# Issue order of weight transfers in a decoder step: the next chunk's sum ahead of a further chunk's load

## The chip, the cores and the metric

The kernel runs on one core of a Trainium2 chip. The metric is the device time of one execution in microseconds (us). Several executions are timed, and the median counts. One more execution is recorded by the hardware profiler; all rows shown here are from such a recording.

The names are those of the profile: PE is the matrix engine, with PEld for its weight loads; DVE, ACT and POOL are the vector, scalar and GpSimd engines; SP is the engine that here only issues transfers. SPq and POOLq are transfers issued by SP and POOL. L191 is line 191 of the kernel before.

## The reference, cut to what matters

The reference is one inference step of a two-layer decoder for 512 prompt tokens and 8 sample tokens, all in fp32, with model width 1024. Each layer is

```
x = x + 0.5 * swiglu(rmsnorm(x), w_gate, w_up, w_down)
x = x + mixer(rmsnorm(x))        # layer 0: causal pooling, layer 1: window attention
x = x + 0.5 * swiglu(rmsnorm(x), w_gate, w_up, w_down)
swiglu(h) = (silu(h @ w_gate) * (h @ w_up)) @ w_down      # 1024 -> 2816 -> 1024
```

The keys and values of the attention are projected once from x after layer 0. The four feed-forward blocks (FFN 0 to 3) are nearly all of the work and hold nearly all of the weights.

## The kernel before, in words

All 520 tokens are kept on the chip as columns, in two halves of 260. The weights stream through once. For the precision of fp32, every weight block is split into a high and a low part: ACT writes the high part `wh` (L260), DVE writes the rest `wl` (L261), and a product is three matmuls, high times high, high times low and low times high, each of 128 x 128 by 260 columns. L533 is the matmul of plain tiles, L561 that of Strassen tiles.

An FFN has 22 tiles of 128 hidden columns, in parts of 8, 8 and 6. After each part its share of the down projection follows. The first tiles of every FFN (4, 3, 2 and 3) are plain. The other tiles take one step of Strassen's scheme (in Winograd's form): seven products instead of eight. The up and gate blocks of the tile are the two rows of a 2 x 2 matrix of weight blocks, and the seven products need four sums of such blocks: S1 = A21 + A22, S2 = S1 + A11, S4 = A12 + S2 in this kernel's signs, S3 = A11 + A21. The second parts of FFN 0 and FFN 1 also do their down projection so ("woven", because the pieces of neighbouring tiles alternate; 4 tiles of two column blocks each). All other down projections are plain, in 4 chunks.

The weights come through the class `Weights` in a plan written out ahead: a list of chunks (up to 1 MB each, one tile or one pair of column blocks) and a list of pieces in the order in which PE uses them. `_split` walks along the pieces, some five ahead of PE (`prefetch`):

- `load(c)` issues the transfers of chunk c from DRAM into one of 3 buffers `raw`, on SP. The buffer's previous user must be done.
- `add_up(c)` does the sums of a chunk which transfers can do (`loaded`, L187 to L192); for plain chunks it does nothing. On SP it loads one 256 KB block of the chunk a second time, into a tile S (4 rotating buffers, which some other tiles use too). On POOL it issues two accumulating transfers: L191 adds a block of `raw` to S, giving S1, and L192 adds A11 to A21 in place, giving S3. L191 must wait for the load of S and for that of the chunk, L192 for the chunk alone.
- DVE forms S2 (L197, which reads S) and S4 (L201) in place when their piece comes.
- Then ACT and DVE split the piece (L260, L261), and `_split` issues the load of a further chunk and the sum of the next one (L263 to L265).

`held` is true where one of the next two pieces still belongs to an earlier chunk; this is so at the Strassen tiles, whose last piece (A22) is used only after the next tile has begun. `slow` holds the second tile of a woven down projection.

The order of instructions on each engine isn't only that of the program: the framework schedules the instructions by a timeline of its own, within the limits of their dependences. The weight loads are pinned to the order of the program (`later`), as are some other instructions.

The lines to know beside these are: L317 and L318, the high and low part of activations; L332, the issue of every weight transfer on SP; L694 to L706, ACT's and DVE's copies and sums `sa` and `sb` in a Strassen tile; L725 to L752, the same in a woven down projection; L1220 to L1235, the copies of the new keys and values (`vtok` among them) at the start of FFN 2; L1355 to L1500, the attention, of which L1412 transposes the softmax.

Of the kernel before, what the change touches and what calls it, by code (L numbers as in the profile page):

```python
# [126 lines left out]
class Weights:  # L127
# [113 lines left out]
    def _split(self, i):  # L241
        nc = self.nc
        while self.ns <= min(i, len(self.items) - 1):
            it = self.items[self.ns]
            self.load(it[0])
            self.add_up(it[0])
            src = it[1](self.chunks[it[0]][1])
            n = src.shape[1]
            if it[2] is not None:
                dh, dl = it[2]()  # L250
                wh = wl = None
            else:
                wh = self.splp.tile([P, 4, P], F32R, tag="wh", name="wh")
                wl = self.splp.tile([P, 4, P], F32R, tag="wl", name="wl")
                dh, dl = wh[:, :n, :], wl[:, :n, :]
            if len(src.shape) == 4:
                dh = dh.rearrange("p k (e d) -> p k e d", e=2)
                dl = dl.rearrange("p k (e d) -> p k e d", e=2)
            pin = self.pin if wh is not None else self.pin_home
            pin(nc.scalar.activation(dh, src, AF.Copy))  # L260
            pin(nc.vector.tensor_tensor(dl, src, dh.bitcast(F32), op=ALU.subtract))  # L261
            it[2] = (wh, wl)
            held = any(c < it[0] for c, _, _ in self.items[self.ns + 1 : self.ns + 3])  # L263
            self.load(it[0] + self.ca - held)
            self.add_up(it[0] + 1 - (held and it[0] in self.slow))  # L265
            self.ns += 1

    def get(self):
# [1591 lines left out]
```

## Time and profile before

| | before |
|---|---|
| median of 3 runs | 1685.05 us (1684.97 to 1687.89) |
| profiled execution | 1681.19 us |
| its span, first to last instruction | 1679.4 us |
| granted PE clock, mean | 0.994 |
| HBM read | 182.40 MB, 112 GB/s over the span |
| SP's loads of raw, gate | x87, 512 KB, median 4.0 us from issue to landing |
| SP's loads of raw, up | x87, 512 KB, median 5.7 us |
| SP's loads of S | x76 of 256 KB from w_up, 5.6 us |
| POOL's accumulations L192 (raw) | x84, 256 KB, 3.4 us |

How to read the rows: in a timeline the columns are start (us from the first instruction), duration, engine, line, operation, tiles written and read, and in brackets the idle time of the engine just before, with what ended it. In the waits, a row names the waiting engine and line, then what it waited for, the total, the times and the longest. In a row by stretch (start:end) follow its length, then for PE, PEld, DVE, ACT and POOL the busy time and the number of instructions, the granted PE clock as a share of full speed, the share of the transfer engines and GB/s. A transfer that POOL or SP issues takes little of the issuing engine's time, unless the engine has to wait first.

### The profile page before, as it was taken

Reading aid. Unit: us, or ns where it says so; the run is one execution under the profiler, and the core shown is the slowest. Engines: PE = TensorE matmul, PEld = TensorE weight load, DVE = VectorE, ACT = ScalarE, POOL = GpSimd, SP = SyncE. Lnnn points to the kernel's source line nnn. Section 1 sums busy time; section 2 is a strip of 40 time slices with the busy share of each in tenths; the row PEclk is TensorE's granted clock in tenths of the full one; section 3 lists DMA queues with packets and bytes.
Section 4 is the critical chain, followed back from the end, with each engine's and each line's share of the span. In section 5 each row is a group of like instructions: output and inputs, shape, how many; then the busy total and the mean of one; then the engine's idle time right before and its main releaser. Section 6 shows DMA issues by size and latency. Waiting matters only on the chain.

```text
span 1679.4 us, 34587 instructions
## 1 busy us (share of the span) xinstructions
PE 1648.1 (98%) x13674; PEld 1634.9 (97%) x13674; DVE 1287.0 (77%) x2475; ACT 909.9 (54%) x1834; POOL 179.9 (11%) x240
## 2 busy tenths in 40 slices
PE   9999999999999999999999999999989999999997
PEld 9999999999999999999999999999989999999997
DVE  6866989887875998888775875886787785785776
ACT  5643655556652664655552552655785653463455
POOL 0101111000101111100201101101210100110100
PEclk9999999999999999999999999999999999999999
DMA  8646768752655777743755755653222554674641
GB/s 215 139 121 137 175 167 176 178 163 79 139 147 133 173 167 172 167 132 93 172 146 133 167 154 133 151 154 85 66 52 76 133 139 132 146 176 127 147 122 52
DMA packets 329646, 232.27 MB, mean 138 GB/s; under 512 B 10494, under 2 KB 303078, under 8 KB 329444
## 3 DMA queue, kind: packets, MB, share of 16 engines
q1 hardware_dynamic: 300414, 179.96, 38.1%
q0 software_dynamic: 25312, 45.02, 16.3%
q10 hardware_dynamic: 3758, 5.09, 1.0%
q8 instruction: 107, 1.75, 0.5%
q14 instruction: 55, 0.45, 0.1%
HBM read 182.40 MB, written 5.04 MB: 112 GB/s over the span
## 4 chain that ended last, share of the span: by engine, by line
PE 89%; DVE 3%; ACT 3%; DMA 2%; issue 2%; SPq 0%; POOL 0%; ACTq 0%; DVEq 0%; POOLq 0%
PE ps L561 47%; PE ps L533 36%; DMA S<-raw 1%; DVE wl L261 1%; DMA pr<-in_bands_dram 1%; PE ps L1075 1%; PE ps L1443 1%; DMA S<-in_ffn_w_down_dram 1%; ACT sm L1387 1%; ACT wh L260 1%; PE ps L1050 0%; PE ps L1412 0%; PE ps L1734 0%; ACT xh L317 0%; PE ps L1355 0%
## 5 line engine op out<-in xcount | busy, mean ns | idle before, releaser
L260 ACT ACTIVATE wh<-raw 128x512 fp32r<-128x512 f32 (+1 forms) x746 | 447.5, 621 | 455.6 <-PE ps L533 255.8
L261 DVE TENSOR_TENSOR wl<-raw,wh 128x512 fp32r<-128x512 f32 (+1 forms) x746 | 491.5, 677 | 164.5 <-ACT wh L260 161.4
L561 PE MATMUL ps<-th,wh 128*128 128x260 f32 x1216 | 344.4, 283 | 1.8 <-ACT sa L699 0.8
L561 PE MATMUL ps<-tl,wh 128*128 128x260 f32 x1216 | 342.7, 282 | 0.0
L561 PE MATMUL ps<-th,wl 128*128 128x260 f32 x1216 | 340.9, 282 | 0.2 <-DVE wl L261 0.2
L561 PEld LDWEIGHTS ps<-th,wh 128*128 128x128 f32 x1216 | 228.5, 188 | 3.5 <-DVE sb L706 1.4
L561 PEld LDWEIGHTS ps<-tl,wh 128*128 128x128 f32 x1216 | 229.0, 188 | 0.0
L561 PEld LDWEIGHTS ps<-th,wl 128*128 128x128 f32 x1216 | 227.9, 188 | 0.4 <-DVE wl L261 0.4
L533 PE MATMUL ps<-hh,wh 128*128 128x260 f32 x1084 | 219.2, 284 | 0.6 <-ACT vtok L1230 0.6
L533 PE MATMUL ps<-hl,wh 128*128 128x260 f32 x1084 | 219.1, 282 | 0.0
L533 PE MATMUL ps<-hh,wl 128*128 128x260 f32 x1084 | 217.7, 282 | 0.0
L192 POOL DMA_DIRECT2D raw<-raw x84 | 72.4, 862 | 1207.5 <-DVE wl L261 431.7
L561 PE MATMUL ps<-xh,wh 128*128 128x260 f32 x704 | 198.0, 283 | 0.5 <-ACT sb L696 0.5
L561 PE MATMUL ps<-xl,wh 128*128 128x260 f32 x704 | 197.5, 282 | 0.0
L561 PE MATMUL ps<-xh,wl 128*128 128x260 f32 x704 | 195.0, 282 | 0.0
L533 PEld LDWEIGHTS ps<-hh,wh 128*128 128x128 f32 x1084 | 166.5, 188 | 1.5 <-ACT vtok L1230 0.9
L533 PEld LDWEIGHTS ps<-hl,wh 128*128 128x128 f32 x1084 | 167.5, 188 | 0.0
L533 PEld LDWEIGHTS ps<-hh,wl 128*128 128x128 f32 x1084 | 167.0, 188 | 0.0
L533 PE MATMUL ps<-xl,wh 128*128 128x260 f32 x736 | 149.7, 284 | 0.3 <-DVE xl L949 0.3
L533 PE MATMUL ps<-xh,wh 128*128 128x260 f32 x736 | 149.1, 285 | 0.0
L533 PE MATMUL ps<-xh,wl 128*128 128x260 f32 x736 | 148.1, 283 | 0.0
L561 PEld LDWEIGHTS ps<-xh,wh 128*128 128x128 f32 x704 | 132.4, 188 | 0.9 <-ACT sb L696 0.9
(325 smaller groups left out, 3186.8 us busy)
## 6 DMA issues: line engine op xcount, KB each, us to landing
raw<-in_ffn_w_gate_dram SPq DMA_DIRECT2D x87, 512.0 KB, 4.0
raw<-in_ffn_w_up_dram SPq DMA_DIRECT2D x87, 512.0 KB, 5.7
raw<-in_ffn_w_down_dram SPq DMA_DIRECT2D x24, 1024.0 KB, 4.8
raw<-raw POOLq DMA_DIRECT2D x84, 256.0 KB, 3.4
S<-raw POOLq DMA_DIRECT2D x84, 256.0 KB, 4.4
S<-in_ffn_w_up_dram SPq DMA_DIRECT2D x76, 256.0 KB, 5.6
raw<-in_ffn_w_down_dram SPq DMA_DIRECT2D x16, 768.0 KB, 4.4
raw<-in_ffn_w_down_dram SPq DMA_DIRECT2D x32, 256.0 KB, 3.9
```

The lines of the kernel that those rows point to most:

```text
L192: G.dma_start(blk(raw, 2, 1), blk(raw, 1, 1), accum_op=ALU.add)
L260: pin(nc.scalar.activation(dh, src, AF.Copy))
L261: pin(nc.vector.tensor_tensor(dl, src, dh.bitcast(F32), op=ALU.subtract))
L533: ins = T.matmul(banks[:, hf, :H], a[:, kk, :], hcols(b, hf), start=(first and i == 0), stop=(last and i == 2),)
L561: T.matmul(bank[:, :H], a[:, kk, :], b, start=(not more and kk == 0 and i == 0), stop=(kk == 3 and i == 2), skip_group_check=more,)
L1075: T.matmul(po[:, half * 256 : half * 256 + 256], z[:, tau, c], b, start=(i == 0), stop=(i == len(lst) - 1),)
L1387: S.activation(z, z, AF.Exp, scale=-1.0, bias=nm[:, i : i + 1], accum_out=self.den[:, i : i + 1])
L1443: T.matmul(po[:, bi * 256 : (bi + 1) * 256], a, p_[:, kc_], start=(n == 0), stop=(n == 3 * len(kts) - 1),)
```

## The change

In `_split` the sum of the next chunk is asked for before the load of the further chunk, except that a sum is never asked for before its own chunk has been loaded (the `min`); what that leaves over is asked for behind the load, as before.

```diff
             held = any(c < it[0] for c, _, _ in self.items[self.ns + 1 : self.ns + 3])
+            sums = it[0] + 1 - (held and it[0] in self.slow)
+            self.add_up(min(sums, self.nl - 1))
             self.load(it[0] + self.ca - held)
-            self.add_up(it[0] + 1 - (held and it[0] in self.slow))
+            self.add_up(sums)
             self.ns += 1
```

The instructions are the same. Between Strassen tiles the sum stands ahead of the load already, since `held` puts the load off. What moves are 22 of the 84 sums: two at each of the ten places where plain chunks give way to Strassen chunks, and one, that of the third tile, in each of the two woven down projections. Around a change from plain to Strassen chunks, SP's order was load c+1, S of c, load c+2, S of c+1, S of c+2; it is S of c, load c+1, S of c+1, load c+2, S of c+2. On POOL, L191 of a moved sum goes ahead of L192 of the next chunk. In the woven projections the S of the third tile goes ahead of the four transfers that load the fourth. The framework's schedule also moves some instructions of ACT, DVE and PE: within and behind the woven projections, at the starts of FFN 1 and FFN 2, and in the attention.

## The prediction

> **What bounds the kernel now.** I read the page first, then PE's waits grouped by line, then all instructions on the tiles named S (the block of weight sums), then the timelines of the places where PE's waits lead.
>
> ```profile
> span 1679.4 us, 34587 instructions
> PE 1648.1 (98%) x13674; PEld 1634.9 (97%) x13674; DVE 1287.0 (77%) x2475; ACT 909.9 (54%) x1834; POOL 179.9 (11%) x240
> PE 89%; DVE 3%; ACT 3%; DMA 2%; issue 2%; SPq 0%; POOL 0%; ACTq 0%; DVEq 0%; POOLq 0%
> S<-raw POOLq DMA_DIRECT2D x84, 256.0 KB, 4.4
> ```
>
> PE's waits (us in total, times, longest), and from the view of S how long and how often an instruction on S sat idle for that transfer:
>
> ```profile
> PE ps L561 <- ACT wh L260: 2.4, 3, 1.9
> PE ps L561 <- DVE raw L197: 2.3, 1, 2.3
> PE ps L561 <- ACT sa L699: 0.8, 2, 0.6
> PE ps L561 <- DVE sb L706: 0.8, 2, 0.5
> DMA S<-raw: 44.7, 14
> ```
>
> PE is busy 1648.1 of 1679.4 us, and the change neither adds nor removes an instruction. The last row of the first fence gives 4.4 us from issue to landing for the accumulating transfer. So only PE's 31.3 idle us, and any time at a lower clock, can be won; everything else could only be lost. The two largest waits of the Strassen matmuls (L561) end with a split (L260) and with the sum S2 (L197), both readers of an S tile. The last row says that instructions on S tiles sat idle 14 times for S<-raw. There are 84 such transfers and the change moves 22 of their loads. Of these 22 the timelines of ACT and DVE show a split that starts when its S lands at three places only: 252.69, 643.75 and 808.14. The other moved sums lie 3 us or more in front of their splits, or PE does not wait.
>
> **The first place, FFN 0's woven down projection** (timelines of SP, POOL, ACT and PE; columns are start and duration, and the bracket is the idle time before it and its releaser):
>
> ```profile
> 230.21 13.39 SPq L332 DMA_DIRECT2D raw<-in_ffn_w_down_dram  x8
> 241.58 2.02 SPq L332 DMA_DIRECT2D raw<-in_ffn_w_down_dram  x4
> 243.64 1.58 SPq L332 DMA_DIRECT2D S<-in_ffn_w_down_dram  x2
> 249.13 0.86 POOL L191 DMA_DIRECT2D S<-raw  x1 [1.74 <-DMA S<-in_ffn_w_down_dram]
> 252.69 0.63 ACT L260 ACTIVATE wh<-S 128x512 fp32r<-128x512 f32 x1 [7.83 <-DMA S<-raw]
> 251.19 0.28 PE L561 MATMUL ps<-ph,wl 128*128 128x260 f32 x1
> 253.38 0.39 PE L561 MATMUL ps<-hh,wh 128*128 128x260 f32 x1 [1.91 <-ACT wh L260]
> 255.03 0.28 PE L561 MATMUL ps<-hh,wl 128*128 128x260 f32 x1
> 235.00:245.00 10.00, 10.00 (x86) 10.00 (x85) 9.74 (x19) 6.84 (x15) 0.86 (x1) 1.00 0.41 98
> ```
>
> The third tile's sum is queued on SP behind the fourth tile's load (four transfers, issued only at 241.58, when a raw buffer comes free). It therefore starts at 243.64; POOL can accumulate onto it at 249.13, ACT splits at 252.69, and PE stops. At full work PE does 86 matmuls in 10 us, 0.116 each. From 251.19 to 255.03 it makes 7 steps in 3.84 us: 7 x 0.116 = 0.8, so **3.0 us** are lost.
>
> The change puts this sum ahead of the fourth tile's load. It waits then for nothing that is late: it follows the first four transfers of the x8 row, about 230.2 + 2.0 = 232.2. With the same lags (243.64 to 249.13 is 5.5; L191 to landing 4.4 by the page) it has landed by about 242.5, nine us before PE needs it. The load behind it starts at 241.58 as before, since the buffer, not SP, holds it.
>
> **The second place, FFN 1's woven down projection:**
>
> ```profile
> 620.92 13.41 SPq L332 DMA_DIRECT2D raw<-in_ffn_w_down_dram  x8
> 634.38 1.23 SPq L332 DMA_DIRECT2D S<-in_ffn_w_down_dram  x2
> 640.38 1.75 POOL L191 DMA_DIRECT2D S<-raw  x2 [2.31 <-DMA S<-in_ffn_w_down_dram]
> 643.75 0.63 ACT L260 ACTIVATE wh<-S 128x512 fp32r<-128x512 f32 x1 [8.18 <-DMA S<-raw]
> 641.88 0.28 PE L561 MATMUL ps<-ph,wl 128*128 128x260 f32 x1
> 644.44 0.39 PE L561 MATMUL ps<-hh,wh 128*128 128x260 f32 x1 [2.28 <-DVE raw L197]
> 645.10:648.50 3.40, 3.32 (x14) 3.02 (x15) 3.40 (x7) 1.12 (x3) 0.00 (x0) 0.50 0.25 68
> 648.50:651.90 3.40, 3.40 (x31) 3.40 (x30) 2.80 (x6) 2.84 (x7) 0.00 (x0) 1.00 1.14 309
> ```
>
> It is the same pattern, and a second loss follows. From 641.88 to 645.10 PE starts 4 matmuls in 3.2 us: 3.2 - 4 x 0.116 = 2.75 lost. Then the granted clock is 0.50 for 3.4 us, with 14 matmuls against 31 in the next 3.4: 17 x 0.11 = 1.9 lost. Together **4.6 us**. Here an idle stretch of 2.28 us was followed by the half clock; at 253.38 one of 1.91 us was not.
>
> [...]
>
> **Knock-on.** Behind the woven stretch of FFN 0 the next tiles' sums stay late:
>
> ```profile
> 311.06 0.63 ACT L260 ACTIVATE wh<-S 128x512 fp32r<-128x512 f32 x1 [3.49 <-DMA S<-raw]
> 313.05 0.39 PE L561 MATMUL ps<-th,wh 128*128 128x260 f32 x1 [0.60 <-ACT sa L699]
> 317.73 0.39 PE L561 MATMUL ps<-th,wh 128*128 128x260 f32 x1 [0.55 <-DVE sb L706]
> ```
>
> The two L699/L706 waits (0.8 + 0.8 in PE's waits) and the pipeline refills behind them come to at most 2.7 us. These chunks' loads wait for the split of an A22 piece two chunks back, which comes earlier after the change. The transfers there are themselves slower than the 4.4 median, so lateness may build up again. Bounds 0 and 2.7; I take **1.0**, nearer to nothing because the cause, crowded transfers, isn't removed.
>
> **The 20 other sums (ten places where plain tiles give way to Strassen tiles).**
>
> ```profile
> L332 SPq DMA_DIRECT2D S<-in_ffn_w_up_dram x76: 557/1094/2763, 35.6 to 1594.8; - x76
> ```
>
> Each takes some 1.1 us of SP (the median of that row, of 0.56 to 2.76) ahead of a chunk's load, and its POOL accumulate goes ahead of the next chunk's L192. No row of PE's waits ends with a raw load; the loads have that much to spare, so I count nothing; (d) below is the price if they had not. But the scheduler orders ACT and DVE by its own estimate, and in two stages their order changes.
>
> *FFN 2's start.* The split of S goes ahead of the two copies L1230, for which PE waits:
>
> ```profile
> 782.12 0.37 SPq L332 DMA_DIRECT2D raw<-in_ffn_w_gate_dram  x1
> 794.29 1.51 SPq L332 DMA_DIRECT2D S<-in_ffn_w_up_dram  x1
> 800.96 1.21 POOL L191 DMA_DIRECT2D S<-raw  x1
> 799.32 0.58 ACT L1230 COPY vtok<-ps 128x512 f32<-128x512 f32 x1 [0.21 <-PE ps L1229]
> 801.48 0.51 PE L533 MATMUL ps<-hh,wh 128*128 128x260 f32 x2 [0.62 <-ACT vtok L1230]
> 808.14 0.63 ACT L260 ACTIVATE wh<-S 128x512 fp32r<-128x512 f32 x1 [4.51 <-DMA S<-raw]
> ```
>
> After the change this sum is issued behind the load at 782.12, near 783.2, not at 794.29: 11.1 us earlier, so the S that was ready at 808.14 should be ready at about 797, or earlier, before ACT reaches the split at 799. PE then waits some 0.63 (the split) longer, with its refill **+0.8** (bounds 0 and 9.4, the latter below).
>
> *Attention.* A split of the queries (L317/L318) moves behind other work where ACT and DVE are the limit:
>
> ```profile
> 1233.03 1.30 PE L1412 MATMUL ps<-ident,sm 128*128 128x128 f32 x5 [1.15 <-ACT oT L1462]
> 1232.20:1239.00 6.80, 5.97 (x32) 5.69 (x34) 6.49 (x22) 6.40 (x19) 1.61 (x2) 0.50 0.00 1
> ```
>
> I followed the new order by hand with the durations of the rows: about **+0.7** at the matmul of 1233.03. The stretch at half clock may move with it, so bounds are -1.5 and +2.5.
>
> **Sum**, against the profiled execution (1681.19 us, span 1679.4 and 1.8 around it): -3.0 - 4.6 - 1.0 + 0.8 + 0.7 = -7.1, 1674.1. That execution lies 3.86 below the median of the runs, 1685.05, so the forecast for the median is **1678.0** (-0.4%).
>
> **Rivals.**
>
> *(a) Half is given back to DVE.*
> ```profile
> 245.00:255.00 10.00, 7.79 (x61) 7.17 (x60) 6.77 (x13) 2.31 (x5) 2.58 (x3) 1.00 0.82 179
> 255.00:265.00 10.00, 10.00 (x86) 10.00 (x85) 9.97 (x20) 4.88 (x11) 1.75 (x2) 1.00 0.74 169
> ```
> DVE is busy 9.74 and 9.97 of 10 us around the first gap. Over 235 to 265 it has 26.48 us of work; without the lost 3.0 it must do this in 27.0. That just fits, but any misorder makes wl (L261) or the sum S4 (L201) the next late input. Half of 7.6, no knock-on, and the +1.5: -2.3, so 1682.8.
>
> *(b) The sum doesn't come earlier,* because its S tile, one of four that rotate, is still held by an earlier reader, or POOL's queue holds the accumulation. Then PE's gaps stay and the +1.5 remains: 1686.6. Against it: in the changed program this load waits for two earlier transfers only, and no compute engine.
>
> *(c) Slower: FFN 2's start blocks ACT.* Should the scheduler's order put the split of S ahead of L1230 while S lands as late as before, ACT (in order) stands from 799.3 to 808.14 and PE waits for vtok: 8.8 + 0.6 = 9.4 us, and the pause brings the half clock, as in the row of 1232.20, where 6.8 us hold 32 matmuls instead of some 58: about 3.0. -7.1 - 0.8 + 9.4 + 3.0 = +4.5, so 1689.5. It decides if S becomes ready later than about 804, some 7 us behind what I expect. For it: POOL's accumulation of this S, issued at 800.96, took some 7 us to land. Against it: the 11.1 us.
>
> *(d) The further load pays.* If the loads had no room, 22 issues of 1.1 us each would come to 24 us more than the -7.1: 1702. None of PE's waits quoted above speaks for it. [...] In the stretch of the first gap DMA has 0.82 of a full share, and no run here shows the load's loss.
>
> **How the numbers follow.** Forecast 0.64; (a) 0.18; (b) 0.06; (c) 0.09; (d) 0.03. About 0.2% (3.4 us) is what a measurement of this kernel can tell from no change: faster is under 1681.7, slower over 1688.4. The forecast's case and a quarter of (a) are faster: 0.69. The rest of (a) and (b) are within: 0.19. (c) and (d): 0.12. The range: low end with the full knock-on (2.7), no loss at FFN 2 and the attention at -1.5: 1681.19 - 7.6 - 2.7 - 1.5 + 3.86 = 1673.3, so 1673; the high end takes in (a) with some of its spread, 1685.5. It leaves out (b), (c) and (d), 0.18.
>
> **What would show it.** Right: in the profile after, no `DMA S<-raw` wait before the third tile's split near 250 and 640, S issued near 232 and 622, PE without gaps over 1 us there, and no half clock at 645. FFN 2: an S load near 783 and PE's wait for L1230 below 1.5 us. Wrong: a DVE-released gap in the same stretches (a), a gap of 9 us at 800 (c), or PE waits that end with raw loads (d). The forecast fails, too, if new half-clock stretches arise in the attention, each worth about 1.9.

## The result, and the profile after

| | before | after |
|---|---|---|
| median of 7 runs each, one beside the other | 1684.97 us (1682.05 to 1688.17) | 1677.11 us (1674.27 to 1680.75) |
| profiled execution | 1681.19 us | 1677.03 us |
| its span | 1679.4 us | 1675.3 us |
| granted PE clock, mean | 0.994 | 0.993 |

The ratio is 0.9956, with a 95% interval of 0.9939 to 0.9972: faster by 4.7 to 10.3 us. The two profiled spans are only 4.1 us apart. That difference is taken up below, since it decides how the terms are to be read.

The page of the kernel after, and from its view of S how long and how often an instruction on S sat idle for the accumulating transfer (44.7 us, 14 times before). From L263 on all line numbers are higher by 2.

```profile
span 1675.3 us, 34582 instructions
...
PE 1648.2 (98%) x13674; PEld 1636.7 (98%) x13674; DVE 1285.7 (77%) x2475; ACT 910.3 (54%) x1834; POOL 179.7 (11%) x240
...
PE 91%; DVE 3%; ACT 2%; DMA 2%; issue 1%; SPq 0%; POOL 0%; ACTq 0%; DVEq 0%; POOLq 0%
```

```profile
DMA S<-raw: 13.8, 8
```

PE's busy time is the same to 0.1 us; what went is idle time. **FFN 0's woven projection**, in the timelines of SP, POOL and ACT, and PE by stretch:

```profile
232.25 0.45 SPq L334 DMA_DIRECT2D S<-in_ffn_w_down_dram  x1
241.50 2.17 SPq L334 DMA_DIRECT2D raw<-in_ffn_w_down_dram  x4
```

```profile
238.22 0.86 POOL L191 DMA_DIRECT2D S<-raw  x1 [2.74 <-DMA S<-in_ffn_w_down_dram]
```

```profile
244.67 0.63 ACT L260 ACTIVATE wh<-S 128x512 fp32r<-128x512 f32 x1
```

```profile
245.00:255.00 10.00, 10.00 (x86) 10.00 (x85) 10.00 (x21) 4.03 (x9) 2.04 (x3) 1.00 0.97 238
```

The third tile's S starts at 232.25 instead of 243.64. The load that now stands behind it still starts when the raw buffer is free: at 241.50, against 241.58. ACT splits S with no bracket behind it, so nothing was waited for, and PE starts 86 matmuls in the ten us in which it started 61 before. DVE is busy for all of these ten us and holds nothing up.

**FFN 1's**, the same views:

```profile
621.88 1.51 SPq L334 DMA_DIRECT2D S<-in_ffn_w_down_dram  x1
```

```profile
634.31 0.63 ACT L260 ACTIVATE wh<-S 128x512 fp32r<-128x512 f32 x1
```

```profile
635.00:645.00 10.00, 10.00 (x86) 10.00 (x85) 10.00 (x20) 4.09 (x8) 1.72 (x2) 1.00 0.97 241
641.90:648.50 6.60, 6.60 (x57) 6.57 (x55) 5.31 (x11) 2.98 (x6) 1.75 (x2) 1.00 0.68 147
```

No gap, and a granted clock of 1.00 where before had 0.50.

The framework also orders ACT, DVE and PE anew at these places. PE's order is the same up to its 2042nd record, and the one that waited 1.91 us for the split of S is the 2041st (253.38 before; 251.22 after, with no wait). In FFN 1 it is the 5211th (2.28 us before, none after), and the order is the same up to the 5212th. So these two waits did not go by another order on PE.

**Where the 4.1 us of the two spans come from.** The starts of the same matmul in both traces, counted from the first record on PE:

| record on PE | before | after | after - before | what lies ahead of it |
|---|---|---|---|---|
| 2001st | 246.52 | 246.44 | -0.1 | |
| 2301st | 285.48 | 282.47 | -3.0 | FFN 0's woven projection |
| 3041st | 376.50 | 372.45 | -4.1 | the last part of FFN 0 |
| 3101st | 385.90 | 384.74 | -1.2 | start of the pooling mixer |
| 5181st | 638.40 | 637.25 | -1.2 | the plain and Strassen tiles of FFN 1 |
| 6001st | 741.66 | 736.13 | -5.5 | FFN 1's woven projection |
| 9801st | 1195.76 | 1190.28 | -5.5 | FFN 2 |
| 10241st | 1255.80 | 1251.80 | -4.0 | attention |
| 13601st | 1657.30 | 1653.31 | -4.0 | FFN 3 |

The two places gave 4.0 and 4.4 us. Two others took back 2.9 and 1.5: the pooling mixer and the attention. In the former PE waits for the column sums in both kernels (1.13 us before, 1.23 after), but after the change a stretch at half clock follows. The timeline of PE and PE by stretch in the kernel after (the last row lies in the attention, where before had half clock too, 3.41 us at 1211.70 and 6.83 at 1232.18):

```profile
374.55 1.64 PE L494 MATMUL ps<-ones,acc 128*128 128x1 f32 x10 [1.23 <-DVE acc L483]
```

```profile
375.23:382.06 6.83, 6.83 (x34) 6.83 (x34) 2.82 (x15) 2.58 (x9) 0.86 (x1) 0.50 0.50 174
1201.26:1204.67 3.41, 3.41 (x18) 3.41 (x18) 3.41 (x10) 1.62 (x6) 0.17 (x1) 0.50 0.00 0
```

Is that a cost of the change, or of the execution that was recorded? And are the two woven places the whole gain? The experiments ask both.

### The profile page after: what moved, and what is told of

Same layout as the page of the kernel before. It is cut to its first block, busy times and chain, and to the rows that moved or that the text cites. A ratio compares the mean times of both kernels' runs of the same rounds, so it can differ in the third digit from the quotient of the medians.

```text
span 1675.3 us, 34582 instructions
## 1 busy us (share of the span) xinstructions
PE 1648.2 (98%) x13674; PEld 1636.7 (98%) x13674; DVE 1285.7 (77%) x2475; ACT 910.3 (54%) x1834; POOL 179.7 (11%) x240
## 4 chain that ended last, share of the span: by engine, by line
PE 91%; DVE 3%; ACT 2%; DMA 2%; issue 1%; SPq 0%; POOL 0%; ACTq 0%; DVEq 0%; POOLq 0%
PE ps L563 48%; PE ps L535 37%; DMA S<-raw 1%; PE ps L1445 1%; PE ps L1052 1%; PE ps L1077 1%; DVE wl L261 1%; ACT sm L1389 0%; PE ps L1357 0%; PE ps L1736 0%; DMA S<-in_ffn_w_down_dram 0%; PE ps L494 0%; PE ps L1414 0%; ACT xh L319 0%; PE ps L932 0%
## 5 line engine op out<-in xcount | busy, mean ns | idle before, releaser
L535 PE MATMUL ps<-hh,wh 128*128 128x260 f32 x1084 | 219.3, 284 | 0.6 <-ACT vtok L1232 0.6
L535 PE MATMUL ps<-hl,wh 128*128 128x260 f32 x1084 | 219.3, 283 | 0.0
L535 PE MATMUL ps<-hh,wl 128*128 128x260 f32 x1084 | 217.9, 283 | 0.0
L192 POOL DMA_DIRECT2D raw<-raw x84 | 72.4, 862 | 1192.7 <-DVE wl L261 481.1
L535 PEld LDWEIGHTS ps<-hh,wh 128*128 128x128 f32 x1084 | 166.6, 188 | 1.5 <-ACT vtok L1232 0.9
L535 PEld LDWEIGHTS ps<-hl,wh 128*128 128x128 f32 x1084 | 167.6, 189 | 0.0
L535 PEld LDWEIGHTS ps<-hh,wl 128*128 128x128 f32 x1084 | 167.1, 188 | 0.0
L535 PE MATMUL ps<-xl,wh 128*128 128x260 f32 x736 | 149.8, 284 | 0.3 <-DVE xl L951 0.3
L535 PE MATMUL ps<-xh,wh 128*128 128x260 f32 x736 | 149.2, 285 | 0.0
L535 PE MATMUL ps<-xh,wl 128*128 128x260 f32 x736 | 148.1, 283 | 0.0
```

The costliest lines, as they stand in the source:

```text
L192: G.dma_start(blk(raw, 2, 1), blk(raw, 1, 1), accum_op=ALU.add)
L535: ins = T.matmul(banks[:, hf, :H], a[:, kk, :], hcols(b, hf), start=(first and i == 0), stop=(last and i == 2),)
```

## The experiments

My theory: the two sums of the woven projections (2 of the 22 that move) are the gain, because SP stood at the raw buffer's wait in front of them; the other 20 give and take nothing. Rivals: the gain is spread over the sums; the loads behind them pay; it is the bytes in front of the sum that count, not the wait; one stall removed only moves to another place.

Since half-clock stretches come and go (one of 6.83 us at 375.23 after, none there before), I compare stretches between two given matmuls beside the medians: "FFN 0" from the 2001st to the 3041st record on PE, "pooling" from there to the 5181st, "FFN 1" from there to the 6001st, "attention" from the 9801st to the 10241st. (Where a kernel has matmuls of its own, the same ones of before are taken.)

| kernel | FFN 0 | pooling | FFN 1 | attention | median us | runs |
|---|---|---|---|---|---|---|
| before | 129.98 | 261.90 | 103.26 | 60.03 | 1684.97 | 7 |
| before_again | 133.21 | 261.62 | 100.91 | 66.05 | 1687.34 | 1 |
| places_only | 133.58 | 261.93 | 101.49 | 60.57 | 1685.85 | 12 |
| behind_one | 130.84 | 262.84 | 101.04 | 60.96 | 1684.05 | 12 |
| fill_stall | 130.70 | 264.69 | 103.84 | 66.35 | 1689.16 | 12 |
| woven_ffn0 | 126.28 | 263.04 | 103.15 | 64.29 | 1676.14 | 9 |
| woven_ffn0_b | 126.09 | 261.76 | 103.26 | 58.87 | 1676.44 | 6 |
| woven_ffn1 | 132.04 | 265.07 | 98.13 | 59.29 | 1677.24 | 6 |
| woven_ffn1_b | 131.94 | 261.24 | 98.13 | 61.63 | 1679.24 | 7 |
| woven_only | 126.04 | 263.18 | 98.13 | 60.10 | 1676.07 | 6 |
| woven_only_b | 125.81 | 261.52 | 98.13 | 60.12 | 1678.85 | 10 |
| after | 126.01 | 264.80 | 98.88 | 61.51 | 1677.11 | 7 |
| pool_queue | 126.25 | 261.48 | 99.13 | 61.69 | 1678.90 | 11 |
| after_fill | 126.12 | 266.38 | 98.21 | 62.78 | 1676.72 | 6 |

The medians of before beside these runs lay between 1685.0 and 1687.2.

**Which of the moved sums count.** In woven_only the sum goes first at the two woven places alone, in places_only at the ten others alone (against the kernel before; in places_only the condition is `not in`):

```diff
+            sums = it[0] + 1 - (held and it[0] in self.slow)
+            if it[0] in self.slow:
+                self.add_up(min(sums, self.nl - 1))
             self.load(it[0] + self.ca - held)
-            self.add_up(it[0] + 1 - (held and it[0] in self.slow))
+            self.add_up(sums)
```

> The sum goes ahead of the load only in the two woven down projections (2 of the 22 moved sums); at the ten other places the order is that of before. My theory, that these two sums are the whole gain: the PE stalls near 253 us (3.0 us) and 644 us (2.5 us and the half clock behind it, 1.9) are gone, knock-on about -0.9; median near 1677, as after the whole change. Rival, that the gain is spread over the moved sums: 2/22 of 7.9 us, median near 1684.3.

> The sum goes ahead of the load only at the ten places where plain tiles give way to Strassen tiles (20 of the 22 moved sums); in the woven down projections the order is that of before. My theory: no PE wait ended with one of these sums, so the stalls near 253 and 644 us stay and the median is that of before within 2 us, 1683 to 1687. Rival, gain spread over the sums: 20/22 of 7.9 us, median near 1678. Second rival, the loads behind them pay: slower than before, over 1688.

Measured: woven_only 0.9934 of before (0.9911 to 0.9958), places_only 1.0002 (0.9986 to 1.0019). Two sums are the whole gain, and 20 are worth nothing that can be measured (the interval leaves room for some 2.4 us of gain or 3.2 of loss): the rival of the spread gain and that of the paying loads both fall. The stretches say the same: FFN 0 and FFN 1 are short in every kernel that moves their sum, and in no other that leaves it behind the load on SP.

**Is SP's wait the cause, or the bytes in front of the sum?** In behind_one the sum goes behind the first of the four transfers that load the fourth tile (`begin(1)` issues that one). In pool_queue SP keeps its order of before, but POOL issues the sums' loads of the woven projections, so that they pass SP's wait.

```diff
# behind_one
+            sums = it[0] + 1 - (held and it[0] in self.slow)
+            if it[0] in self.slow and not held and self.nl == it[0] + 2:
+                self.begin(1)
+                self.add_up(min(sums, self.nl - 1))
             self.load(it[0] + self.ca - held)
-            self.add_up(it[0] + 1 - (held and it[0] in self.slow))
+            self.add_up(sums)
# pool_queue
-                    tiles.append((ch, W.combos(ch, ld(lambda t: t, d3[:, lo, cols[1]]))))
+                    tiles.append((ch, W.combos(ch, lambda t, s=d3[:, lo, cols[1]]: nc.gpsimd.dma_start(t, s))))
```

> In the woven down projections the sum goes behind the first of the four transfers that load the fourth tile, instead of behind all four (before) or ahead of all (after); the ten other places are as before. That first transfer waits for the raw buffer. My theory, that the sum is late because SP stands at that wait: it starts at about 242.1 and 632.8 us, only 1.5 us earlier than before, and the two stalls shrink by 1.5 us each (to about 1.5 and 1.0), with or without the half clock of 1.9: median 1680 to 1682. Rival, that the sum is late because of the bytes in front of it: three quarters of the bytes are gone from in front of it, so three quarters of the gain, median near 1679.

> SP's order is that of before, but the sums' loads of the two woven down projections are issued by POOL instead of SP, so they don't stand behind SP's wait for the raw buffer. My theory, that the wait at the head of SP's queue makes the sum late and not its place among the bytes: the third tile's sum starts near 236 and 625 us, both stalls go, median 1676 to 1679 as after the change. Rival, that the order against the chunk's load matters in itself (bandwidth): no gain. POOL can lose too: if a load waits at the head of POOL's queue, the accumulations behind it come late and the stall stays.

The timelines of SP and of PE in behind_one:

```profile
229.84 11.74 SPq L336 DMA_DIRECT2D raw<-in_ffn_w_down_dram  x5
241.62 0.51 SPq L336 DMA_DIRECT2D S<-in_ffn_w_down_dram  x1
242.17 1.96 SPq L336 DMA_DIRECT2D raw<-in_ffn_w_down_dram  x3
```

```profile
251.79 0.39 PE L565 MATMUL ps<-hh,wh 128*128 128x260 f32 x1 [0.69 <-ACT wh L260]
...
253.32 0.39 PE L565 MATMUL ps<-hh,wl 128*128 128x260 f32 x1 [0.51 <-DVE wl L261]
```

With three quarters of the bytes gone from in front of it the sum still starts at 241.62, since the first transfer stands at the wait. The steps on PE are 0.97 and 0.78 us there instead of 0.12: 1.5 us lost where 1.5 were expected and three quarters of the gain would have left 0.75. In FFN 1 it is 1.65 instead of the 1.0 expected. The median missed: 1684.05, 0.9986 of before (0.9969 to 1.0003), where 1680 to 1682 had been expected. In the last part of FFN 0 this kernel lost 3.7 us at six waits between 291 and 330 us, against 1.9 at three in before: the knock-on grew and ate what the stall gave.

In pool_queue, the timelines of POOL and ACT:

```profile
229.08 0.78 POOL L389 DMA_DIRECT2D S<-in_ffn_w_down_dram  x1 [2.56 <-DVE raw L197]
237.28 0.91 POOL L191 DMA_DIRECT2D S<-raw  x1
```

```profile
243.66 0.63 ACT L260 ACTIVATE wh<-S 128x512 fp32r<-128x512 f32 x1
```

SP issues the eight raw transfers in one row as before (229.12, 13.52 us), but the third tile's S, which POOL asks for at 229.08 (near 236 had been expected), was loaded by then, and both stalls are gone: 0.9956 (0.994 to 0.9971), the ratio of the change itself. What made the sum late was the wait at the head of the queue that it stood in. On POOL's queue, where 2.56 us of idle lay ahead of it (it was issued at 229.08), it was early enough.

The 20 sums that moved ahead of loads gave and cost nothing that can be measured (places_only: 1.0002). The sum behind SP's wait started 11.4 us later than the one ahead of it (243.64 in before, 232.25 in after).

**One place at a time.** The sum goes first in the woven projection of FFN 0 alone, or of FFN 1 alone (the condition is `it[0] == min(self.slow)`, or its opposite within `self.slow`), each run twice, with woven_only once more beside the second runs.

> The sum goes ahead of the load only in the woven down projection of FFN 0. My theory: the stall of 3.0 us near 253 goes and about 0.9 us of the waits behind it; the stall near 641 us and the half clock behind it stay; median near 1681.1, half way. Rival, that one stall only moves to a later place (the DVE limit, or the next late sum): within 1 us of before.

> The sum goes ahead of the load only in the woven down projection of FFN 1. By the first profile it should give 2.5 us for the stall, and 1.9 where the half clock follows: median 2.5 to 4.5 us below before. By the run with FFN 0 alone, which took most of the whole gain, only about 2 us are left for FFN 1. If the two places add up, this run and that one together give the gain of both.

> The run woven_ffn0 once more, beside its counterparts on one chip. In the profiles so far the FFN 0 stretch costs 4 to 7.5 us more with the late sum than without (6.0 on average), the FFN 1 stretch 2.8 to 5 (3.7). My theory, that the two places are independent: this kernel lies about 6 us below before and about 3.7 above woven_only_b. Rival, that either place alone gives nearly everything, as the first runs with one place suggest: within 1.5 us of woven_only_b.

> The run woven_ffn1 once more. My theory (independent places): about 3.7 us below before and 6 above woven_only_b; its FFN 0 stretch in the profile is 4 us or more longer than that of woven_ffn0_b, its FFN 1 stretch about 98 to 99 us. Rival: within 1.5 us of woven_only_b.

> The run woven_only once more: 8 to 11 us below before, no stall at either place. It is the yardstick for the two runs beside it.

The stretches are as independent as the theory has it. Over the profiles with the sum behind the whole load on SP (before, before_again, places_only, and the two runs of the kernel that leaves this place as it was), FFN 0 takes 132.2 us on average and 126.0 with the sum ahead (the kernels of the change and its parts): **6.1 us**. FFN 1 takes 102.4 and 98.3: **4.1 us**. In the kernel with one place, the other still has its stall; here PE in woven_ffn1_b, its timeline and by stretch:

```profile
253.42 0.39 PE L564 MATMUL ps<-hh,wh 128*128 128x260 f32 x1 [2.21 <-ACT wh L260]
```

```profile
255.21:258.62 3.41, 3.41 (x18) 3.41 (x17) 3.05 (x6) 0.65 (x2) 0.00 (x0) 0.50 0.63 180
```

and in woven_ffn0_b:

```profile
640.07 0.39 PE L564 MATMUL ps<-hh,wh 128*128 128x260 f32 x1 [1.97 <-DVE raw L197]
```

```profile
641.57:644.98 3.41, 3.41 (x17) 3.41 (x17) 3.40 (x7) 0.66 (x2) 0.00 (x0) 0.50 0.50 144
```

The whole times don't add up so. Against before, woven_ffn0 was 0.9943 (0.9923 to 0.9963) and 0.9939 (0.992 to 0.9957), woven_ffn1 0.994 (0.9919 to 0.9961) and 0.9955 (0.9937 to 0.9972), both together 0.9934 and 0.9952 (0.9934 to 0.997). From the stretches 1680.4 and 1682.4 were to be expected for one place (1686.5, the mean of the 64 runs of before beside them, less 6.1 or 4.1); the means of all runs are 1677.4 (15 runs) and 1678.5 (13). By the totals the rival is right, by the stretches my theory. The next section has possible reasons, which are not shown.

**Was the first profile a lucky one?** The kernel before, unchanged:

> The kernel before, unchanged, profiled again. If the first profile was a favourable execution (1681.2 against a median near 1686 over many runs), this one shows longer stalls near 250 and 640 us, or more stretches at half clock, and their sum makes up the difference of the two times. Rival: the time differs with no change in stalls and clock.

SP, POOL and PE in its timelines, and two stretches:

```profile
243.21 1.06 SPq L332 DMA_DIRECT2D S<-in_ffn_w_down_dram  x2
```

```profile
250.35 0.86 POOL L191 DMA_DIRECT2D S<-raw  x1 [4.14 <-DMA S<-in_ffn_w_down_dram]
```

```profile
254.49 0.59 PE L561 MATMUL ps<-hh,wh 128*128 128x260 f32 x1 [3.75 <-ACT wh L260]
```

```profile
253.70:260.50 6.80, 6.01 (x25) 5.70 (x26) 5.60 (x10) 3.91 (x9) 0.00 (x0) 0.50 0.61 149
1246.97:1260.63 13.66, 13.66 (x69) 13.21 (x69) 8.35 (x35) 6.97 (x28) 3.19 (x4) 0.50 0.33 72
```

It was. The same S, issued at nearly the same time (243.21 against 243.64), was ready for POOL 7.1 us later instead of 5.5. PE idled 3.75 us instead of 1.91, and half clock followed at FFN 0, not at FFN 1. The execution took 1687.34 us, 6.2 more than the first one: +3.2 in FFN 0, -2.4 in FFN 1, +6.0 in the attention, between -0.7 and +0.4 elsewhere. The half clock in the pooling mixer, too, comes and goes with the execution: in one of woven_only that stretch took 263.18 us with it, in another 261.52 without. So that one in the profile after need not be a cost of the change.

**The half clock.** In fill_stall, with the order of before, PE gets 8 matmuls on a tile of ones (16 records in the profile, two for each) ahead of the product that waits; in after_fill, after the change, 5 ahead of the column sums of the pooling mixer.

```diff
# fill_stall (the products on either side are pinned to the program's order)
+            fill(c[:, 1, :], 8 if i == 2 else 0, later)
             product(b["T1"], c[:, 1, :])
# after_fill: in rstd_tok, called with more=5 in the pooling mixer
+        fill(pss_[0][:, 1, :], more)
         for t, lo in enumerate(tiles):
```

> The order of before, with 8 matmuls on a tile of ones (their sums are overwritten) put on PE just ahead of the product that waits for the late sum, in both woven down projections; some 1.8 us of PE work inside a stall that lasts 2 us or more. The stalls themselves stay. My theory, that the half clock behind these stalls follows from PE's idle time and is about 2 us of the loss, in one of the two places in most executions: no half clock at 250 to 262 or 640 to 652 us, adjusted time 1 to 3 us below before. Rival, that the half clock there has another cause: it still appears in one of the two places, and the time is that of before or up to 1 us longer.

> The kernel after the change, with 5 matmuls on a tile of ones put on PE ahead of the five column sums (L492 of before) in the pooling mixer, where PE sits idle for 0.8 to 1.5 us. In the profiles so far the stretch from there to the second woven projection costs 261.2 to 261.9 us without a half clock and 263 to 265 with one. My theory, that idle PE time brings the half clock: with the idle time filled, no half clock follows there and this stretch takes 261 to 262 us; the median lies 0 to 2 us below after, whose spread from the attention stays. Rival, that it comes for another reason: a half clock there in the profile, or the stretch at 263 us or more.

The timeline of PE in fill_stall, and one stretch:

```profile
250.67 1.95 PE L527 MATMUL ps<-ones 128*128 128x128 f32 x16
252.88 0.39 PE L561 MATMUL ps<-hh,wh 128*128 128x260 f32 x1 [0.26 <-ACT wh L260]
...
644.87 1.95 PE L527 MATMUL ps<-ones 128*128 128x128 f32 x16
648.09 0.39 PE L561 MATMUL ps<-hh,wh 128*128 128x260 f32 x1 [1.28 <-DVE raw L197]
```

```profile
649.40:652.81 3.41, 3.41 (x15) 3.41 (x16) 3.41 (x7) 0.84 (x2) 0.00 (x0) 0.50 0.44 126
```

Where the fill covered the stall (0.26 idle left) no half clock came; in FFN 1, where the wait was longer and 1.28 us were left idle behind the same 16 records, it did. That fits idle time as the cause, but one place each is little. What came is what the rival had named: a half clock at one of the two places, and a time that did not fall: 1.0012 of before (0.9997 to 1.0027), with 264.69 us in the pooling and 66.35 in the attention (261.90 and 60.03 in before), at a granted clock of 0.988 against 0.994. The forecast of 1 to 3 us failed, and the cause of the half clock stays open.

The fill in after_fill missed its aim. The framework put it and the next group's products ahead of the column sums. The wait of 1.23 us in front of these went, but a later one, 0.46 us in the kernel after, became 2.94, and half clock begins inside it:

```profile
372.18 1.28 PE L530 MATMUL ps<-ones 128*128 128x128 f32 x10
...
381.05 0.58 PE L1053 MATMUL ps<-th,xh 128*128 128x256 f32 x1 [2.94 <-DVE zl L323]
```

```profile
379.60:386.43 6.83, 5.38 (x25) 5.38 (x26) 4.20 (x10) 3.66 (x10) 0.00 (x0) 0.50 0.46 168
```

The pooling stretch took 266.38 us, the longest of all, and the median is that of the change: 1676.72, 0.9937 of its own before (0.9918 to 0.9955). No kernel of these is better than the change by more than the runs can tell.

## Why the prediction was right, step by step

The forecast was 1678.0, the measured median 1677.11. The mechanism was right; several sizes were not, and they cancelled.

- **The first place.** S at 232.2 forecast, 232.25 measured; no wait of ACT or PE left; the load behind it not delayed. Right. Of size it was the term that was most underrated: 3.0 with a knock-on of 1.0, from a profile in which the stall was small. In that pair it gave 4.0, but over the profiles 6.1, with the half clock that followed in some of them (at 253.70 in before_again, at 255.21 in woven_ffn1_b).
- **The second place.** Right, and the half clock behind it too: 4.6 forecast, 4.4 in the pair, 4.1 on average. The 1.9 for the half clock was read as part of the stall, and no chance was given to it. It came in some executions at the one place, in some at the other (at 645.09 in before, at 253.70 in before_again).
- **Knock-on.** 1.0 forecast, 1.0 in the pair (after less before goes from -3.0 at 303 us to -4.0 at 333). Two waits of PE stay in that part. Here the kernel after:

```profile
309.66 0.39 PE L563 MATMUL ps<-th,wh 128*128 128x260 f32 x1 [0.70 <-ACT sa L701]
...
314.51 0.36 PE L563 MATMUL ps<-th,wh 128*128 128x260 f32 x1 [0.26 <-DVE sb L708]
```

- **The 20 other sums at nothing.** Right: places_only, 1.0002.
- **FFN 2's start.** 0.8 forecast, 0.2 measured: the gap at L1231 (L1229 before) grew from 0.22 to 0.41, that at L535 stayed at 0.62. The timelines of SP, ACT and PE after:

```profile
777.63 0.87 SPq L334 DMA_DIRECT2D S<-in_ffn_w_up_dram  x1
```

```profile
793.48 0.61 ACT L260 ACTIVATE wh<-S 128x512 fp32r<-128x512 f32 x1
794.00 0.56 ACT L1232 COPY vtok<-ps 128x512 f32<-128x512 f32 x1
```

```profile
794.62 0.65 PE L1231 MATMUL ps<-ident,vT 128*128 128x128 f32 x4 [0.41 <-ACT vtok L1232]
...
796.14 0.51 PE L535 MATMUL ps<-hh,wh 128*128 128x260 f32 x2 [0.62 <-ACT vtok L1232]
```

  S was there long before, as forecast, and its split filled the time in which ACT had waited for PE. Rival (c), which needed S late, had no ground.
- **Attention.** +0.7 forecast, +1.5 in the pair, which shows nothing: before itself took 60.0 and 66.1 us there in two executions, and the 61.5 of the kernel after lies between. The order of ACT and DVE there is another in nearly every kernel, so the others don't settle what the new order costs. I read an order where two executions of one kernel lie 6.0 us apart.
- **Rival (a), DVE.** DVE was busy all ten of ten us at both places and PE still had no gap, so the work just fits, as worked out.
- **The offset of 3.86 us** between the profiled execution and the median was carried along as if it held for both kernels. That was luck: after the change the profiled execution was at its median. Before the change it was not: that execution had a small stall (1.91 us, against 3.75 in before_again) and few half clocks (a granted clock of 0.994, against 0.989), so the medians lie 7.9 us apart and the spans 4.1. The forecast of -7.1 for the profile was 3.0 too much there, 2.9 of it in the pooling mixer, where a half clock came that no step foresaw.

What stays open is why one place alone brings nearly the whole gain in the total. In the profiles the totals differ, beside the two stretches, mostly by the pooling and the attention, and the attention's time went with its place on the grid described below. A stall that goes shifts all later places on that grid (the 9801st matmul starts 5.5 us earlier after the change). Besides, woven_ffn0 and woven_ffn1 have one order of ACT and DVE in the attention, which neither before nor woven_only has. Whether either of the two favoured the kernels with one place was not tried.

## What to carry to other kernels

On SP a transfer that waited for a buffer held back the S queued behind it, independent as it was, to 243.64 instead of 232.25. In another kernel, look on the issuing queue for a long row whose issue is stretched by a wait, and ask which of the transfers behind it is needed first. Putting that one ahead cost nothing here, since the blocked transfer was bound by its buffer anyway (241.50 instead of 241.58). Before a stall is priced, profile the kernel a second time; and compare kernels of a similar time by stretches between the same instructions, not by one pair of spans.

## What the runs showed of the hardware

**In these profiles half clock came in steps of 3.41 us, on a grid that is not tied to the kernel.** Stretches at half clock inside the span were one, two or four times 3.41 us long (3.41 at 645.09 and 6.83 at 1232.18 in before, 13.65 at 1246.97 in before_again), and within an execution their starts lay whole multiples of that step apart (566.61 us from 645.09 to 1211.70 in before, 166 steps of 3.413; 242 steps from 375.23 to 1201.26 in after). The place of the grid differed between two executions of one kernel: counted back in this step to the start of the span, it lies at 3.4 us in before and at 1.1 in before_again. A stall of 1.91 us that lay over a border of the grid (252.56, 115 of these steps back from 645.09) left about 1.1 idle on either side and brought none; one of 2.28 within a step did, and so did 1.28 with another 0.29 behind it. But idle time in one step does not decide it alone. In places_only a step in which PE was busy for only 1.53 of 3.41 us was followed by full clock:

```profile
643.70:647.11 3.41, 1.53 (x13) 1.32 (x11) 0.36 (x1) 0.35 (x1) 1.45 (x2) 1.00 0.76 132
647.11:650.53 3.42, 2.78 (x18) 2.37 (x19) 3.42 (x8) 2.14 (x6) 0.00 (x0) 1.00 0.18 33
```

and in the kernel after the step ahead of the half clock at 375.23 was a busier one:

```profile
371.82:375.23 3.41, 2.18 (x20) 2.01 (x18) 2.50 (x5) 2.05 (x5) 0.00 (x0) 1.00 1.32 400
```

What decides stays open: the step ahead of 375.23 in after had 1.23 us idle and the one ahead of 645.09 in before 2.29, and half clock followed both; the one of places_only had 1.88, and full clock followed.

**In these profiles the attention's time went with its place on that grid.** Ordered by the time from the last border of the grid to the 9801st matmul, the attention stretch took 66.4 to 64.3 us from 0.14 to 0.36, 60.6 to 60.0 from 0.52 to 1.13, 58.9 to 59.3 between 1.63 and 1.93, and 61.0 to 61.7 from 2.24 to 2.68, in 13 of the 14 profiles; after_fill stands apart with 62.8 at 1.96. PE's order is the same there in all of them, that of ACT and DVE is not. But profiles that share all three orders differ just so: before with 60.0 at 1.13 and 66.1 at 0.26; woven_ffn0 and woven_ffn1, two profiles each, with 64.3 at 0.36, 58.9 at 1.63, 59.3 at 1.93 and 61.6 at 2.24. In woven_only_b a spread of over 10 us between executions (1671.55 to 1682.93) came with a granted clock of 0.995 at its fast end and 0.990 at its slow one.
